# Four reorderings in a one-core encoder layer: values' copies before the next split, a pair's transposes in one run, an earlier conv mean, and first factors by ScalarE

## The chip, the cores and the metric

The kernel runs on one core of one Trainium2 chip. The metric is the device time of one execution in microseconds (us). Engines are named as in the profile: PE is TensorE (PEld its weight loads), DVE is VectorE, ACT is ScalarE, POOL is GpSimd, SP is SyncE, which issues most DMAs.

## The reference, cut to what matters

One hybrid encoder layer over 512 positions of width 2048, all float32. Names are those of the reference.

```python
xn = rms_norm(x, attn_norm_g[l])
proj = xn @ w_in[l]
u_val, u_gate, q, k, v = split(proj)              # 1024 columns each
y_conv = conformer_conv(u_val, u_gate, ...)       # u_val*sigmoid(u_gate) -> depthwise conv of 31
                                                  # -> layer norm over channels -> silu
y_na = neighborhood_attention(q, k, v, rpb[l])    # 16 heads of 64, 8 x 64 grid, windows of 8 x 16
mixed = concat([rms_norm(y_conv), rms_norm(y_na)])
x = x + mixed @ w_out[l]
up = depthwise_conv(rms_norm(x) @ w_up[l])        # width 3, 2 x 5632 columns
x = x + (silu(gate) * val) @ w_down[l]
return rms_norm(x, final_norm_g)
```

## The kernel before, in words

**Products.** Nearly all the time is matrix products. A product keeps float32 accuracy by three matmuls: each factor is split into a high part in the reduced type float32r and a low part, and `mm3` (L124 to L129) adds high by high (L127), low by high (L128) and high by low (L129) into one PSUM bank. Weights arrive by SP's DMAs in units of 128 x 1024 (`raw`). `parts` (L113 to L118) splits a unit: ACT copies the high part (`whi`, L116), and DVE subtracts for the low part (`wlo`, L117). There are four buffers of each, and `weights()` prepares units three ahead, so the split of a later unit waits until PE has read the last of an earlier one.

**Stages.** At the start the kernel loads the input and the first weights piece by piece, scales and splits them, and begins the first conv group's product. ACT and DVE share that work; the factors `g1` of the first norm are copied by DVE (L263). Then a list `ORDER` runs the input projections: conv groups ("a"), two halves of the values ("v"), and pairs of heads ("q"). A unit of a projection is eight rows of weights, that is 24 matmuls. `project_v` (L310 on) fills four PSUM banks with the values of one half; ACT then copies each bank to SBUF twice or three times, aligned and shifted (`vg` L335, `vx` L338). The first half uses three of the banks that projections use, so the next projection has to wait for the first bank's copies.

**Steps in between.** Attention and the conv group's norm are generators in the lists `steps` and `asteps`. `tick` (L136 to L144) is called after each unit and lets each list go one step further. A pair of heads goes through `scores` (into PSUM), `softmax` (tables `tab`), `turn` and `values`. `turn` (L496 to L509) transposes four tables, 16 transposes on PE (L503) in four groups of four, in the order n = 2, 3, 0, 1, and ACT copies each group out (`pt`, L508). Groups 2 and 3 have a PSUM tile each; groups 0 and 1 are the two halves of one tile, `wide`, allocated in the middle of the loop. `group_a` (L389 on) makes the conv group's mean (two matmuls, L396), subtracts it (L401), and sums squares for `rsqrt_steps` (matmuls L190 and L207); its factor `ra` is copied out of PSUM by ACT (L213) before `read_a` (L599 on) can empty the banks of the first output products (`out_half`, `po` in the profile).

**What sets the order.** The program is written in one sequence. A planner puts each engine's instructions into a queue, by their place in the program (which `shifted` moves), by what they depend on and by its own times; on the chip each engine works its queue in order and waits on semaphores. `tc.issue_after(x)` holds an instruction back behind another in the plan. `pin` (`tc.keep_in_program_order`) keeps an instruction in the order of the program among the pinned ones of its engine. PSUM has eight banks: three for tag `mm`, one for `po` (attention output, norm sums, and the output product with d == 3), two for `tr`, two for `sc`.

The second part of the kernel is the gated MLP (`up`, `down`) and the last norm. Its code is not changed.

Of the kernel before, what the change touches and what calls it, by code (L numbers as in the profile page):

```python
# [12 lines left out]
AF = mybir.ActivationFunctionType  # L13
# [17 lines left out]
KD = D // P  # L31
# [3 lines left out]
U = 8  # L35
# [31 lines left out]
def layer(ctx: ExitStack, tc: tile.TileContext, xT, xG, xw, w_a, w_in, w_v, w_out, w_up, w_down, par, tab, g3, out, last_out):  # L67
    nc = tc.nc
# [21 lines left out]
        return wpool.tile(shape, F32, tag="raw", name=name, bufs=NR)  # L90

    pin = tc.keep_in_program_order

    g1 = consts.tile([P, KD], F32, name="g1")
    prm = consts.tile([P, NPAR], F32, name="prm")
# [17 lines left out]
    def parts(raw, n):  # L113
        hi = wpool.tile([P, U * P], F32R, tag="whi", name="whi", bufs=NW)
        lo = wpool.tile([P, U * P], F32R, tag="wlo", name="wlo", bufs=NW)
        i = nc.scalar.activation(hi[:, :n], raw[:, :n], AF.Copy)  # L116
        j = nc.vector.tensor_sub(lo[:, :n], raw[:, :n], hi[:, :n].bitcast(F32))  # L117
        return hi, lo, i, j  # L118

# [4 lines left out]
    def mm3(ps, w, wk, mh, ml, start, stop):  # L124
        hi, lo = w[:2]
        a = slice(wk * P, (wk + 1) * P)
        nc.tensor.matmul(ps, hi[:, a], mh, start=start, stop=False)  # L127
        nc.tensor.matmul(ps, hi[:, a], ml, start=False, stop=False)  # L128
        return nc.tensor.matmul(ps, lo[:, a], mh, start=False, stop=stop)  # L129


    steps, asteps = [], []

    def tick(behind):
        for todo in (steps, asteps):
            while todo:  # L136
                try:
                    with tc.issue_after(behind.ins):
                        next(todo[0])
                    break  # L140
                except StopIteration:
                    todo.pop(0)
# [86 lines left out]
    ps = psa.tile([P, 2, S], F32, tag="sc", name="idle")  # L229
# [3 lines left out]
    for k in range(KD):  # L233
        if k < CH:
            raw = t4([P, U * P], "raw")
            n = S + 2 * P + (0 if k else KD)
            last = pin(nc.sync.dma_start(raw[:, :n], xw[:, k * (S + 2 * P) + (KD if k else 0):][:, :n]))
            x1.append(raw[:, :S])
            first = raw[:, S:S + 2 * P]
        else:  # L240
            if k % CH == 0:
                raw = t4([P, U * P], "raw")
            if k % CH == 0 or k == CH + 2:
                o, n = 2 * (k % CH) * P, 2 * (2 if k < 2 * CH else CH) * P
                pin(nc.sync.dma_start(raw[:, o:o + n], w_a[:, 2 * (k - CH) * P:][:, :n]))
            x1.append(t2("x"))
            last = pin(nc.sync.dma_start(x1[k], xG[k - CH]))
        h, l = t2("xh", F32R), t2("xl", F32R)
        g = g1[:, k:k + 1] if k else raw[:, n - KD:n - KD + 1]
        if k:  # L250
            pin(nc.scalar.activation(h, x1[k], AF.Copy, scale=g))
        else:
            pin(nc.vector.tensor_scalar(h, x1[k], g, None, op0=ALU.mult))
        pin(nc.vector.scalar_tensor_tensor(l, x1[k], g, h.bitcast(F32), op0=ALU.mult, op1=ALU.subtract))
        xs.append((h, l))
        if k < CH:
            early_parts(first, k)
        elif k % 2 == 0:
            early_parts(raw[:, 2 * (k % CH) * P:2 * (k % CH + 2) * P], k)
        if k in (6, 8, 10, 12):  # L260
            sum_sq(acc1, x1[k // 2 - 3], k == 6)
        if k == 0:
            pin(nc.vector.tensor_copy(g1, raw[:, n - KD:n]))  # L263
    with tc.issue_after(last.ins):
        nc.sync.dma_start(prm, par)
    a_, q_, v_ = iter(range(NC_)), iter(range(NP_)), iter(range(2))
    for step in ORDER:
        if step == "v":
            half = next(v_)
# [3 lines left out]
        i = next(a_ if step == "a" else q_)  # L273
# [22 lines left out]
    def project(n):  # L296
        ps = psm.tile([P, S], F32, tag="mm", name="pj")
        for u in range(KD // U):
            w = weights()
            for k in range(U):  # L300
                kk = u * U + k
                m = mm3(ps, w, k, xs[kk][0], xs[kk][1], kk == 0, kk == KD - 1)
            tick(m)
            while late and rstd:
                late.pop(0)()
        return ps

    vg, vx = [], []

    def project_v(half):  # L310

        if half:
            sc = psa.tile([P, 2, S], F32, tag="sc", name="pv")
            banks = [psa.tile([P, S], F32, tag="tr", name="pv", bufs=2) for _ in range(2)] + [sc[:, 0], sc[:, 1]]
        else:
            banks = [psm.tile([P, S], F32, tag="mm", name="pv") for _ in range(3)]
            banks.append(psa.tile([P, S], F32, tag="po", name="pv"))
        for u in range(KD // 2):
            wh, wl = weights()[:2]
            for k in range(2):  # L320
                kk, f = 2 * u + k, slice(k * S, (k + 1) * S)
                for t, ps in enumerate(banks):
                    xh, xl = (x[:, t * P:(t + 1) * P] for x in xs[kk])
                    nc.tensor.matmul(ps, xh, wh[:, f], start=kk == 0, stop=False)  # L324
                    nc.tensor.matmul(ps, xl, wh[:, f], start=False, stop=False)  # L325
                    m = nc.tensor.matmul(ps, xh, wl[:, f], start=False, stop=kk == KD - 1)  # L326
            tick(m)
            while late and rstd:
                late.pop(0)()
        y = rtok[0]  # L330
        vg.append([t2("vg") for _ in banks])
        vx.append([t2("vx") for _ in banks[1:]])
        with shifted(-600):
            for t, ps in enumerate(banks):
                nc.scalar.activation(vg[half][t], ps, AF.Copy, scale=y[:, t:t + 1])  # L335
                for x, rows in ((t - 1, slice(0, DH)), (t, slice(DH, P))):
                    if 0 <= x < len(vx[half]):
                        nc.scalar.activation(vx[half][x][rows], ps[rows], AF.Copy, scale=y[rows, t:t + 1])  # L338

    def project_first():  # L340

# [47 lines left out]
    def group_a():  # L389
        h, l = t2("yh", F32R), t2("yl", F32R)  # L390
        nc.scalar.activation(h, ysum[0], AF.Copy)
        nc.vector.tensor_sub(l, ysum[0], h.bitcast(F32))
        yield
        ps = psa.tile([P, S], F32, tag="po", name="st")
        for i, m in enumerate((h, l)):
            nc.tensor.matmul(ps, ones_r, m, start=i == 0, stop=i == 1)  # L396
        mu = t2("mu")
        nc.vector.tensor_scalar(mu, ps, 1.0 / CONV, None, op0=ALU.mult)
        acc = t2("acc")
        for i in range(NC_):  # L400
            nc.vector.tensor_sub(ys[i], ys[i], mu)  # L401
            sum_sq(acc, ys[i], i == 0)
            if i == NC_ // 2 - 1:
                yield
        yield
        yield
        r = yield from rsqrt_steps(acc, CONV, "rln")
        acc = t2("acc")
        for i in range(NC_):
            nc.vector.tensor_mul(ys[i], ys[i], r)  # L410
            nc.scalar.activation(ys[i], ys[i], AF.Silu, scale=pc("lng", i), bias=pc("lnb", i))
            ma.append(split(ys[i], pc("cog", i), "ma"))
            sum_sq(acc, ys[i], i == 0)
            if i % 2:
                yield
        yield
        yield
        ra.append((yield from rsqrt_steps(acc, CONV, "ra")))
# [76 lines left out]
    def turn(ts):  # L495
        pts, first = {}, True  # L496
        for n in (2, 3, 0, 1):
            if n == 0:
                wide = psa.tile([P, 2, 4, P], F32, tag="sc", name="trp")
            ps = wide[:, n] if n < 2 else psa.tile([P, 4, P], F32, tag="tr", name="trp", bufs=2)  # L500
            for i in range(2):
                for ch in range(2):
                    m = nc.tensor.transpose(ps[:, 2 * i + ch, :], ts[n][:, i, ch * P:(ch + 1) * P], ident)  # L503
                    if not first:
                        pin(m)
                    first = False
            pts[n] = t2("pt").rearrange("p (c k) -> p c k", c=4)
            nc.scalar.activation(pts[n], ps, AF.Copy)  # L508
        return pts  # L509

    def values(p, pts):
# [39 lines left out]
    p, n = -1, 0  # L551
# [392 lines left out]
    n = CH  # L944
# [47 lines left out]
    for d in range(KD):  # L992
        ps = psm.tile([P, S], F32, tag="mm", name="pd")[:, fm]
# [8 lines left out]
    sums, v, r, y, w = (sm.tile([P, CH], F32, tag="rs" + c, name="rs" + c) for c in "lvryw")  # L1002
    v, r, y, w = (t[:, :1] for t in (v, r, y, w))
# [16 lines left out]
    for g, ps in enumerate(banks):  # L1020
        for i in range(CH):
            m = nc.tensor.matmul(ps[:, i * P:(i + 1) * P], x2[g * CH + i][:, tm], ident, start=i == 0, stop=False,
                                 is_transpose=True)
            if g > 1 and i == 0:
                pin(m)
        for k in range(n):
            (hh, hl), (dh, dl) = hs[k], ws[g * CH + k]
            i = nc.tensor.matmul(ps, hh[:, tm], dh, start=False, stop=False)
# [3 lines left out]
            i = nc.tensor.matmul(ps, hl[:, tm], dh, start=False, stop=False)  # L1032
# [104 lines left out]
```

## Time and profile before

| what | value |
|---|---|
| median of 3 runs | 2025.43 us (2024.95, 2025.43, 2026.96) |
| profiled execution: its time / its span | 2026.78 us / 2025.0 us |
| PE busy in the span | 2013.7 us (99%) |
| DVE busy | 1668.0 us (82%) |
| ACT busy | 1052.0 us (52%) |
| DMA, mean | 140 GB/s |

The profile is of one execution. Its time is 1.8 us longer than its span, which runs from the first to the last recorded instruction. In the timelines, a row begins with the start in us from the span's start and the duration in us, then engine, line, operation, output and inputs, and in brackets how long the engine was idle before it and what ended that. Matmuls overlap: a duration of 0.39 us goes with a start every 0.23 us, so lost time shows in the starts rather than in the busy share.

### The profile page before, as it was taken

Reading aid. Unit: us, or ns where it says so; the run is one execution under the profiler, and the core shown is the slowest. Engines: PE = TensorE matmul, PEld = TensorE weight load, DVE = VectorE, ACT = ScalarE, POOL = GpSimd, SP = SyncE. Lnnn points to the kernel's source line nnn. Section 1 sums busy time; section 2 is a strip of 40 time slices with the busy share of each in tenths; the row PEclk is TensorE's granted clock in tenths of the full one; section 3 lists DMA queues with packets and bytes.
Section 4 is the critical chain, followed back from the end, with each engine's and each line's share of the span. In section 5 each row is a group of like instructions: output and inputs, shape, how many; then the busy total and the mean of one; then the engine's idle time right before and its main releaser. Section 6 shows DMA issues by size and latency. Waiting matters only on the chain.

```text
span 2025.0 us, 28150 instructions
## 1 busy us (share of the span) xinstructions
PE 2013.7 (99%) x10556; PEld 1721.0 (85%) x10556; DVE 1668.0 (82%) x2300; ACT 1052.0 (52%) x1686; POOL 168.7 (8%) x199
## 2 busy tenths in 40 slices
PE   9999999999999999999999999999999999999998
PEld 8788888888888998888888888888888888888887
DVE  7976888988577899888888888888888888879875
ACT  6323344466346555555555555555555555555563
POOL 0000000000001101111111111111111111110111
PEclk9999999999999999999999999999999999999999
DMA  7223333336338765565565565565565565564573
GB/s 257 94 85 93 113 94 106 106 112 231 104 119 214 198 167 146 125 146 146 125 146 146 129 142 146 127 143 146 118 153 146 125 146 146 125 144 127 146 201 132
DMA packets 98935, 284.25 MB, mean 140 GB/s; under 512 B 10992, under 2 KB 12272, under 8 KB 98800
## 3 DMA queue, kind: packets, MB, share of 16 engines
q1 hardware_dynamic: 72144, 231.07, 36.8%
q0 software_dynamic: 26656, 51.39, 16.9%
q8 instruction: 83, 1.36, 0.3%
q14 instruction: 52, 0.43, 0.1%
HBM read 227.89 MB, written 54.53 MB: 139 GB/s over the span
## 4 chain that ended last, share of the span: by engine, by line
PE 98%; DVE 1%; ACT 0%; issue 0%; DMA 0%; ACTq 0%; DVEq 0%
PE pu L759 27%; PE pu L765 14%; PE pd L129 8%; PE pd L127 8%; PE pd L128 8%; PE pj L127 6%; PE pj L129 5%; PE pj L128 5%; PE po L127 3%; PE po L129 3%; PE po L128 3%; PE pv L325 1%; PE pv L324 1%; PE pv L326 1%; PE trp L503 1%; PE pu L127 1%
## 5 line engine op out<-in xcount | busy, mean ns | idle before, releaser
L116 ACT ACTIVATE whi<-raw 128x1024 fp32r<-128x1024 f32 x364 | 384.6, 1058 | 507.8 <-PE pj L128 137.9
L117 DVE TENSOR_TENSOR wlo<-raw,whi 128x1024 fp32r<-128x1024 f32 x364 | 444.4, 1222 | 210.1 <-ACT whi L116 203.3
L759 PE MATMUL pu<-xc,whi 128*128 128x512 f32 x2352 | 580.0, 391 | 0.0
L759 PEld LDWEIGHTS pu<-xc,whi 128*128 128x128 f32 x2352 | 433.5, 188 | 83.0
L765 PEld LDWEIGHTS pu<-xc,wlo 128*128 128x128 f32 x2352 | 306.9, 191 | 14.7
L765 PE MATMUL pu<-xc,wlo 128*128 128x256 f32 x2352 | 311.4, 282 | 0.0
L129 PE MATMUL pd<-hh,wlo 128*128 128x512 f32 x640 | 250.3, 391 | 0.0
L127 PE MATMUL pd<-hh,whi 128*128 128x512 f32 x640 | 249.7, 390 | 0.0
L128 PE MATMUL pd<-hl,whi 128*128 128x512 f32 x640 | 249.1, 389 | 0.0
L913 POOL DMA_DIRECT2D x2d<-pdc x160 | 139.4, 873 | 1097.8 <-ACT pdc L912 870.9
L127 PE MATMUL pj<-xh,whi 128*128 128x512 f32 x512 | 199.6, 394 | 2.3 <-ACT vx L338 2.2
L129 PE MATMUL pj<-xh,wlo 128*128 128x512 f32 x512 | 199.2, 392 | 0.0
L128 PE MATMUL pj<-xl,whi 128*128 128x512 f32 x512 | 198.9, 391 | 0.0
L791 ACT ACTIVATE pl<-pu 128x256 f32<-128x256 f32 x294 | 109.8, 382 | 149.9 <-PE pu L759 142.8
L379 DVE SCALAR_TENSOR_TENSOR y<-ch,prm,y 128x500 f32<-128x500 f32 (+14 forms) x240 | 173.5, 740 | 4.3
L116 ACT ACTIVATE whi<-ws 128x1024 fp32r<-128x1024 f32 x132 | 139.7, 1058 | 70.9 <-PE pu L759 55.2
L117 DVE TENSOR_TENSOR wlo<-ws,whi 128x1024 fp32r<-128x1024 f32 x132 | 161.1, 1221 | 14.8 <-ACT whi L116 14.8
L129 PEld LDWEIGHTS pd<-hh,wlo 128*128 128x128 f32 x640 | 120.1, 188 | 28.5 <-DVE wlo L117 3.3
L128 PEld LDWEIGHTS pd<-hl,whi 128*128 128x128 f32 x640 | 120.2, 188 | 24.9 <-DVE hl L898 0.3
L127 PEld LDWEIGHTS pd<-hh,whi 128*128 128x128 f32 x640 | 120.4, 188 | 22.6
L912 ACT ACTIVATE pdc<-pd 128x512 f32<-128x512 f32 x160 | 93.8, 588 | 79.3 <-PE pd L129 66.2
L127 PEld LDWEIGHTS pj<-xh,whi 128*128 128x128 f32 x512 | 96.6, 189 | 23.5 <-ACT vx L338 2.6
(220 smaller groups left out, 2728.9 us busy)
## 6 DMA issues: line engine op xcount, KB each, us to landing
raw<-in_w_up SPq DMA_DIRECT2D x176, 512.0 KB, 3.8
raw<-in_w_down SPq DMA_DIRECT2D x88, 512.0 KB, 4.0
x2d<-pdc POOLq DMA_DIRECT2D x160, 256.0 KB, 4.9
raw<-in_w_in SPq DMA_DIRECT2D x60, 512.0 KB, 3.8
raw<-in_w_out SPq DMA_DIRECT2D x32, 512.0 KB, 3.7
raw<-in_w_v SPq DMA_DIRECT2D x16, 512.0 KB, 3.7
tab<-in_tab SPq DMA_DIRECT2D x32, 256.0 KB, 5.1
x<-in_xT SPq DMA_DIRECT2D x16, 256.0 KB, 5.4
```

Source lines behind the costliest of these rows:

```text
L116: i = nc.scalar.activation(hi[:, :n], raw[:, :n], AF.Copy)
L117: j = nc.vector.tensor_sub(lo[:, :n], raw[:, :n], hi[:, :n].bitcast(F32))
L127: nc.tensor.matmul(ps, hi[:, a], mh, start=start, stop=False)
L128: nc.tensor.matmul(ps, hi[:, a], ml, start=False, stop=False)
L129: return nc.tensor.matmul(ps, lo[:, a], mh, start=False, stop=stop)
L324: nc.tensor.matmul(ps, xh, wh[:, f], start=kk == 0, stop=False)
L379: nc.vector.scalar_tensor_tensor(y[:, a:b], h[:, a + j - PAD:b + j - PAD], prm[:, o + j:o + j + 1], y[:, a:b], op0=ALU.mult, op1=ALU.add)
L759: i = nc.tensor.matmul(ps, w[0][:, k * P:(k + 1) * P], comb[c][k], start=k == 0, stop=stop and k == ks[-1])
L765: i = nc.tensor.matmul(ps[:, H:], w[1][:, k * P:(k + 1) * P], comb[c][k][:, :H], start=False, stop=stop and k == U - 1)
L791: nc.scalar.activation(to, ps, AF.Copy)
L912: nc.scalar.activation(t, ps, AF.Copy)
L913: nc.gpsimd.dma_start(xd[d], t, accum_op=ALU.add)
```

## The change

Four edits:

1. After the copies of `project_v`, a mark (`copied`) makes the next split of a unit on ACT a pinned instruction. The copies are pinned too, so the copies stand before that split in ACT's queue.
2. After the transposes of `turn`, a mark (`turned`) makes the first matmul of the next `mm3` a pinned one. The transposes of a pair are pinned already, so this matmul comes after all 16.
3. `group_a` yields "mid" after the split of the sum. `project` calls `tick(m, mid=True)` after the fifth row of weights of each unit, and only a step that stands at "mid" is taken there. A third empty `yield` keeps the later steps at the units where they were.
4. `g1` is copied by ACT rather than DVE.

```diff
     pin = tc.keep_in_program_order
+    copied, turned = [], []
...
         i = nc.scalar.activation(hi[:, :n], raw[:, :n], AF.Copy)
+        if copied:
+            copied.pop()
+            pin(i)
...
-        nc.tensor.matmul(ps, hi[:, a], mh, start=start, stop=False)
+        m = nc.tensor.matmul(ps, hi[:, a], mh, start=start, stop=False)
+        if turned:
+            turned.pop()
+            pin(m)
...
-    steps, asteps = [], []
-
-    def tick(behind):
+    steps, asteps, amid = [], [], [False]
+
+    def tick(behind, mid=False):
+
         for todo in (steps, asteps):
-            while todo:
+            while todo and mid == (todo is asteps and amid[0]):
                 try:
                     with tc.issue_after(behind.ins):
-                        next(todo[0])
+                        at = next(todo[0])
+                    if todo is asteps:
+                        amid[0] = at == "mid"
                     break
...
         if k == 0:
-            pin(nc.vector.tensor_copy(g1, raw[:, n - KD:n]))
+            pin(nc.scalar.activation(g1, raw[:, n - KD:n], AF.Copy))
...
                 m = mm3(ps, w, k, xs[kk][0], xs[kk][1], kk == 0, kk == KD - 1)
+                if k == U // 2:
+                    tick(m, mid=True)
             tick(m)
...
-                nc.scalar.activation(vg[half][t], ps, AF.Copy, scale=y[:, t:t + 1])
+                pin(nc.scalar.activation(vg[half][t], ps, AF.Copy, scale=y[:, t:t + 1]))
                 for x, rows in ((t - 1, slice(0, DH)), (t, slice(DH, P))):
                     if 0 <= x < len(vx[half]):
-                        nc.scalar.activation(vx[half][x][rows], ps[rows], AF.Copy, scale=y[rows, t:t + 1])
+                        pin(nc.scalar.activation(vx[half][x][rows], ps[rows], AF.Copy, scale=y[rows, t:t + 1]))
+        copied.append(half)
...
         nc.vector.tensor_sub(l, ysum[0], h.bitcast(F32))
-        yield
+        yield "mid"
...
-        yield
-        yield
+        for _ in range(3):
+            yield
         r = yield from rsqrt_steps(acc, CONV, "rln")
...
             nc.scalar.activation(pts[n], ps, AF.Copy)
+        turned.append(pts)
         return pts
```

## The prediction

> **What bounds the kernel now.** I read the page first (busy times, then the chain that ended last), then the waits of TensorE and of its weight loads, then timelines around the places that the edits touch.
>
> ```profile
> span 2025.0 us, 28150 instructions
> PE 2013.7 (99%) x10556; PEld 1721.0 (85%) x10556; DVE 1668.0 (82%) x2300; ACT 1052.0 (52%) x1686; POOL 168.7 (8%) x199
> ...
> PE 98%; DVE 1%; ACT 0%; issue 0%; DMA 0%; ACTq 0%; DVEq 0%
> ...
> PE pj L127 <- ACT vx L338: 2.2, 1, 2.2
> PEld trp L503 <- ACT pt L508: 2.7, 8, 0.4
> ```
>
> The chain is PE for 98%: nothing counts unless it moves PE's matmuls. Of PE's own waits the one long one is 2.2 us, once, on a values' copy. The last row is a warning: eight times, as many as there are pairs, a weight load for a transpose waited for a copy `pt`. So the edits are priced by what they do to gaps between matmul starts.
>
> **Edit 1, values' copies.**
>
> ```profile
> 87.35 0.39 PE L326 MATMUL pv<-wlo,xh 128*128 128x512 f32 x1
> ...
> 94.15 0.39 PE L326 MATMUL pv<-wlo,xh 128*128 128x512 f32 x1
> 96.73 0.50 PE L127 MATMUL pj<-xh,whi 128*128 128x512 f32 x1 [2.19 <-ACT vx L338]
> ...
> 97.78 0.63 PE L128 MATMUL pj<-xl,whi 128*128 128x512 f32 x1
> ...
> 101.18 0.39 PE L127 MATMUL pj<-xh,whi 128*128 128x512 f32 x1
> 94.35 1.06 ACT L116 ACTIVATE whi<-raw 128x1024 fp32r<-128x1024 f32 x1 [4.38 <-PE pv L325]
> 95.32 0.67 ACT L335 ACTIVATE vg<-pv,rsy 128x512 f32<-128x512 f32 x1
> 96.00 0.68 ACT L338 ACTIVATE vx<-pv,rsy 64x512 f32<-64x512 f32 x1
> 97.80:101.10 3.30, 3.30 (x9) 2.62 (x8) 3.19 (x6) 3.24 (x6) 0.00 (x0) 0.50 0.44 146
> ```
>
> From 87.35 to 94.15 are 30 matmuls, 0.227 us each: the cadence used below. The next was due at 94.38 and started at 96.73, 2.35 late, plus some 0.11 for a first load that nothing covered: 2.46. ACT stood idle for 4.38 us in front of a split that waits for the unit's end, with the copies behind it. The first bank's last matmul starts nine places before 94.15, at 92.11, and ends at 92.50. With the copies ahead, its two (0.67 and 0.68) end near 93.9, before 94.38: the wait goes. The split comes after ten copies, near 99.2 rather than 94.35, and DVE's low part later still; PE needs that unit three units of 24 matmuls after 94.38, at 110.7, so its cover is about ten us. The second half's copies already stand ahead of their split: nothing there.
>
> After the gap the granted clock was 0.50 (third number from the end of the last row), and from 97.78 to 101.18 eight matmuls took 0.425 each: 1.59 us more. The Trainium skill ("TensorE: Matmul & The Clock Gate", "Why this matters for your kernels") asks only that idle gaps stay under about 3 us. By that rule this gap would cost no clock, and the sum below would rise by the 1.59; the trace shows the half clock after a 2.2 us gap, so the row decides.
>
> **Edit 4, first factors.**
>
> ```profile
> 2.03 0.20 ACT L228 ACTIVATE idle<-ones 128x1 f32<-128x1 f32 x1
> 5.58 0.17 DVE L263 COPY g<-raw 128x16 f32<-128x16 f32 x1
> 5.79 0.72 ACT L251 ACTIVATE xh<-raw,g 128x512 fp32r<-128x512 f32 x1 [1.31 <-DVE g L263]
> 6.11 0.62 PE L129 MATMUL pj<-xh,wlo 128*128 128x512 f32 x2
> 6.42 0.40 ACT L223 ACTIVATE whi<-raw 128x256 fp32r<-128x256 f32 x1
> 6.87 0.73 PE L127 MATMUL pj<-xh,whi 128*128 128x512 f32 x2
> raw<-in_xw SPq DMA_DIRECT2D x1, 384.0 KB, 3.8
> ```
>
> After L129 at 6.11 and 6.34 the next matmul was due at 6.57, came at 6.87 and its pair took 0.11 longer: 0.41. On ACT a copy of 128x16 isn't shown; it lies between 0.20 (128x1) and 0.40 (128x256). ACT is free at 4.48 (5.79 less 1.31), so it ends before the second input piece, issued near 1.2, lands near 5.0. Then `xh` starts 0.8 earlier and the split ends near 6.0, before 6.57. Gain 0.41, between 0 and 0.41.
>
> **Edit 3, the mean.**
>
> ```profile
> 433.39 0.39 PE L129 MATMUL pj<-xh,wlo 128*128 128x512 f32 x1
> 433.99 1.05 PE L190 MATMUL st<-ones,acc 128*128 128x1 f32 x8 [0.21 <-DVE acc L170]
> ```
>
> L190 was due at 433.62: 0.37 lost to a sum of squares that DVE finished late. With subtractions and squares up to half a unit (2.7 us) earlier this goes: gain 0.37, between 0 and 0.4.
>
> **Edit 2, transposes.**
>
> ```profile
> 258.07 1.06 ACT L116 ACTIVATE whi<-raw 128x1024 fp32r<-128x1024 f32 x1 [4.38 <-PE pj L128]
> 258.11 1.48 PE L503 MATMUL trp<-ident,tab 128*128 128x128 f32 x12
> 259.04 1.56 ACT L508 ACTIVATE pt<-trp 128x512 f32<-128x512 f32 x3
> 259.34 0.48 PE L127 MATMUL pj<-xh,whi 128*128 128x512 f32 x1
> ...
> 260.65 0.66 PE L503 MATMUL trp<-ident,tab 128*128 128x128 f32 x4
> 261.06 0.48 PE L129 MATMUL pj<-xh,wlo 128*128 128x512 f32 x1
> ...
> 309.31 0.39 PE L127 MATMUL pj<-xh,whi 128*128 128x512 f32 x1
> 309.62 0.66 PE L503 MATMUL trp<-ident,tab 128*128 128x128 f32 x4
> ...
> 307.99 1.58 ACT L508 ACTIVATE pt<-trp 128x512 f32<-128x512 f32 x3 [5.11 <-PE trp L503]
> ```
>
> The last four transposes (n = 1) write the other half of the tile `wide` from which ACT copies n = 0, and they began 0.05 after that third copy ended (259.04 + 1.56 = 260.60, then 260.65; 309.57, then 309.62). Five matmuls of the projection filled the time in the first pair, four in the second. In the changed program PE's queue holds 16 transposes in a row in five pairs (first, second, third, seventh, eighth). ACT's copies stay where they are, so the 13th transpose still begins at 260.65, PE idles 1.2 us from 259.42, and the displaced matmuls follow: after 261.06 the stream is behind by exactly their number. Four pairs by 5 x 0.227 = 1.13, one by 4 x 0.227 = 0.91: 5.44 lost. The joining of two runs saves nothing, as ACT sets the end. Lower bound 0, if the copies came 1.2 earlier; upper bound about 1.3 a pair (6.5). The fourth and fifth pairs keep five matmuls in between.
>
> The sixth pair changes otherwise. Its four last transposes now stand behind the 24 matmuls of the first output product (before: behind 24 of the last key projection), which then come after them. PE's count stays, but two things follow. The sums L207 now stand right behind the third output product, and the fourth, which takes the same single bank `po`, right behind them; ACT's queue holds a split that waits for that third product ahead of the copy `ao`, which frees the bank for L207.
>
> ```profile
> 499.75 0.58 ACT L524 ACTIVATE ao<-po 128x512 f32<-128x512 f32 x1
> 501.10 0.62 PE L207 MATMUL st<-dg,ones 128*128 128x512 f32 x2
> 501.76 0.60 ACT L213 ACTIVATE ra<-st 128x512 f32<-128x512 f32 x1 [0.77 <-PE st L207]
> 502.69 1.07 ACT L116 ACTIVATE whi<-raw 128x1024 fp32r<-128x1024 f32 x1 [0.33 <-PE po L128]
> 502.71 0.39 PE L127 MATMUL po<-mah,whi 128*128 128x512 f32 x1
> ```
>
> Before, `ao` went ahead of that split (499.75, 502.69), and five matmuls lay between L207 and the next user of the bank at 502.71, behind `ra`'s end at 502.36. After: let the third product's last matmul start at t. The high part's last reader ends at t - 0.23 + 0.39; the split starts near t + 0.20, `ao` 0.97 later (as 94.35 to 95.32) and ends 0.60 on, so L207 starts near t + 1.81 instead of t + 0.23: 1.58. The second L207 starts 0.23 after the first and ends 0.39 later; `ra` starts 0.04 after that and takes 0.60; with 0.05 more the fourth product starts 1.08 after the second L207 instead of 0.23: 0.86. Together 2.44, between 0 (if `ao` isn't held) and 3.2 (ACT later by one more 0.7 copy).
>
> **The sum.** Against the profiled execution (2026.78, of which the span is 2025.0 and 1.78 lies outside, unchanged): -2.46 - 1.59 - 0.41 - 0.37 + 5.44 + 2.44 = +3.05, so 2029.8. The runs shown lie at 2024.95 and 2025.43 and at 2026.96; the profiled time is 1.4 to 1.8 above the lower two, about the half clock's 1.59. I estimate that those two ran without it. From the median the sum is then +4.64: 2030.1. I take 2030.0. From the second part of the kernel I expect no change: its chain is PE before and after, and all of it starts later.
>
> **The rivals.**
> - *The half clock follows the new gaps.* For: it followed one of 2.2 us. Against: the five are 1.2, and the sixth pair's 1.58 and 0.86 are parted by two sums. Each time costs 1.59: 2031.6 with the sixth pair alone, up to 2039.5 with five more. By the skill's rule of 3 us it comes at none.
> - *The sixth pair costs nothing,* because ACT reaches `ao` sooner: 2030.0 - 2.44 = 2027.6. Against it stands the queue.
> - *The other side: the 13th transpose no longer waits.* If the third copy ends before the twelfth transpose does, the five runs cost nothing, and the time is 2030.0 - 5.44 = 2024.6, not slower. It decides at 1.2 us: so much earlier must ACT finish. For it: a split fills ACT from 258.07 right ahead of the copies. Against: in the second pair no split did, and the wait ended just as exactly on the copy.
> - *All as the edits say,* nothing lost: 2022.2, not quite 0.2% down.
>
> **How the numbers follow.** Forecast 0.60 (2029.3 to 2030.8); half clock 0.20, of it 0.13 for the sixth pair alone; sixth pair free 0.11; no wait in the runs 0.06; all gained 0.03. The range 2027.5 to 2032.0 holds 0.60 + 0.13 + 0.11 = 0.84. About 0.2% (4.05 us) can be told from no change; slower by more starts at 2029.48. The forecast lies close above it: four fifths of its 0.60 and the half clock's 0.20 give 0.68 slower. Faster by more (under 2021.4) gets 0.02, and 0.30 is left for same.
>
> **What would show it.** (Lines as before the change.) Right: no wait of `pj` on `vx` and clock 1.00 near 98; five new waits of PE transposes on `pt`, about 1.2 each; new waits of `st` L207 on `ao` (1.6) and of the next output product on `ra` (0.9), near 500; `xh` starting near 5.0. Wrong: 16 transposes through in 1.9 us without a gap, or a clock of 0.50 anywhere between 255 and 545.

## The result, and the profile after

| | before | after |
|---|---|---|
| median (range, runs) | 2026.67 us (2024.95 to 2026.96, 9) | 2030.77 us (2029.58 to 2032.02, 9) |
| ratio after / before | | 1.0024, 95% interval 1.0015 to 1.0034 |
| profiled execution: time / span | 2026.78 / 2025.0 us | 2031.87 / 2029.8 us |

The changed kernel is slower by about 4 us, as forecast, and the time lies inside the range. Both kernels' times fall into two groups. Before, three of the nine lie within 0.5 of 2025.2 and six near 2026.7. After, five lie at 2029.58 to 2030.77 and four at 2031.4 to 2032.0. The groups come from the halved TensorE clock, which follows a gap in some executions and not in others: after, the mean granted clock is 0.999 in the five and 0.998 in the four. The two medians come from different groups, the upper one before and the lower one after. Group against group the change costs more than the 4.1 between the medians: 5.6 in the lower (medians 2024.96 and 2030.53) and 5.1 in the upper (2026.70 and 2031.84).

Page of the kernel after: the span, the busy times, the chain that ended last.

```profile
span 2029.8 us, 28156 instructions
PE 2013.8 (99%) x10556; PEld 1721.3 (85%) x10556; DVE 1667.7 (82%) x2299; ACT 1051.5 (52%) x1687; POOL 168.9 (8%) x199
...
PE 99%; ACT 1%; DMA 0%; issue 0%; SPq 0%; DVE 0%; ACTq 0%
```

PE has the same 10556 matmuls and the same busy time (2013.7 before). The 4.8 us of span are gaps and clock, and the waits say where. Waits of PE, after (total us, times, longest):

```profile
PE trp L516 <- ACT pt L521: 5.1, 5, 1.1
PE st L217 <- ACT ao L538: 1.4, 1, 1.4
...
PE po L131 <- ACT ra L223: 0.7, 1, 0.7
```

The wait of `pj` on `vx` (2.2) is gone. In its place stand five waits of the 13th transpose, one of the sums L217 on `ao` and one of the next output product on `ra`. (Lines have moved: transposes L516, `pt` L521, `mm3` L131, L135 and L136, sums L217.)

**The start.** Timeline after:

```profile
4.41 0.20 ACT L273 ACTIVATE g<-raw 128x16 f32<-128x16 f32 x1
5.09 0.72 ACT L261 ACTIVATE xh<-raw,g 128x512 fp32r<-128x512 f32 x1 [0.48 <-DMA raw<-in_xw]
...
6.46 0.63 PE L131 MATMUL pj<-xh,whi 128*128 128x512 f32 x2
...
6.99 0.72 ACT L261 ACTIVATE xh<-raw,g 128x512 fp32r<-128x512 f32 x1 [0.86 <-DMA raw<-in_xw]
...
8.07 0.73 PE L131 MATMUL pj<-xh,whi 128*128 128x512 f32 x2
...
9.69 0.39 PE L131 MATMUL pj<-xh,whi 128*128 128x512 f32 x1
```

The first `xh` starts 0.70 earlier (5.09 for 5.79), but the second waits for its input piece until 6.99. The matmuls are 0.41 ahead of the kernel before at 6.46 and 0.31 at 8.07; at 9.69 (before: 9.78) 0.09 is left.

**The values.** Timeline after, PE and ACT, and a stretch with its busy time and clock:

```profile
94.06 0.39 PE L338 MATMUL pv<-wlo,xh 128*128 128x512 f32 x1
94.28 0.39 PE L131 MATMUL pj<-xh,whi 128*128 128x512 f32 x1
...
93.15 0.69 ACT L350 ACTIVATE vx<-pv,rsy 64x512 f32<-64x512 f32 x1
...
98.96 2.00 ACT L117 ACTIVATE whi<-raw 128x1024 fp32r<-128x1024 f32 x2
96.73:101.10 4.37, 4.37 (x21) 1.00 0.00 0
```

The projection follows the last value matmul at the usual cadence, the split starts at 98.96 (forecast 99.2), and the clock stays at 1.00.

**A pair.** Timeline after, first pair:

```profile
253.89 1.47 PE L516 MATMUL trp<-ident,tab 128*128 128x128 f32 x12
256.43 0.66 PE L516 MATMUL trp<-ident,tab 128*128 128x128 f32 x4 [1.07 <-ACT pt L521]
256.84 0.47 PE L131 MATMUL pj<-xh,whi 128*128 128x512 f32 x1
...
253.86 1.06 ACT L117 ACTIVATE whi<-raw 128x1024 fp32r<-128x1024 f32 x1 [4.38 <-PE pj L135]
254.82 1.56 ACT L521 ACTIVATE pt<-trp 128x512 f32<-128x512 f32 x3
```

ACT's third copy ends at 254.82 + 1.56 = 256.38, and the 13th transpose starts 0.05 later, as before. What has changed is that PE idles for the 1.07 us ahead of it, from the end of the 12th, where projection matmuls stood before.

**The sixth pair.** Timeline after, PE and ACT, then two stretches:

```profile
500.51 0.39 PE L136 MATMUL po<-mah,wlo 128*128 128x512 f32 x1
502.30 0.73 PE L217 MATMUL st<-dg,ones 128*128 128x512 f32 x2 [1.41 <-ACT ao L538]
503.73 0.79 PE L131 MATMUL po<-mah,whi 128*128 128x512 f32 x1 [0.69 <-ACT ra L223]
...
500.71 1.06 ACT L117 ACTIVATE whi<-raw 128x1024 fp32r<-128x1024 f32 x1 [1.78 <-PE po L135]
501.67 0.58 ACT L538 ACTIVATE ao<-po 128x512 f32<-128x512 f32 x1
...
499.93:503.35 3.42, 1.70 (x7) 1.00 0.92 346
503.35:506.76 3.41, 3.04 (x7) 0.50 0.53 159
```

The split does stand ahead of `ao` in ACT's queue, and PE waits first for `ao` (1.41) and then for `ra` (0.69). Then the clock is 0.50 for 3.41 us, in this execution.

### The profile page after: what moved, and what is told of

It is laid out like the page before. It is cut to its first block, busy times and chain, and to the rows that moved or that the text cites. A ratio compares the mean times of both kernels' runs of the same rounds, so it can differ in the third digit from the quotient of the medians.

```text
span 2029.8 us, 28156 instructions
## 1 busy us (share of the span) xinstructions
PE 2013.8 (99%) x10556; PEld 1721.3 (85%) x10556; DVE 1667.7 (82%) x2299; ACT 1051.5 (52%) x1687; POOL 168.9 (8%) x199
## 4 chain that ended last, share of the span: by engine, by line
PE 99%; ACT 1%; DMA 0%; issue 0%; SPq 0%; DVE 0%; ACTq 0%
PE pu L773 26%; PE pu L779 14%; PE pd L136 8%; PE pd L131 8%; PE pd L135 8%; PE pj L131 6%; PE pj L135 6%; PE pj L136 6%; PE po L131 3%; PE po L135 3%; PE po L136 3%; PE pv L337 1%; PE pv L338 1%; PE pv L336 1%; PE po L532 1%; PE pu L131 1%
## 5 line engine op out<-in xcount | busy, mean ns | idle before, releaser
L136 PE MATMUL pd<-hh,wlo 128*128 128x512 f32 x640 | 250.4, 391 | 0.0
L131 PE MATMUL pd<-hh,whi 128*128 128x512 f32 x640 | 249.7, 390 | 0.0
L135 PE MATMUL pd<-hl,whi 128*128 128x512 f32 x640 | 249.1, 389 | 0.0
L131 PE MATMUL pj<-xh,whi 128*128 128x512 f32 x512 | 198.6, 393 | 0.1
L135 PE MATMUL pj<-xl,whi 128*128 128x512 f32 x512 | 198.1, 390 | 0.0
L136 PE MATMUL pj<-xh,wlo 128*128 128x512 f32 x512 | 198.1, 390 | 0.0
L136 PEld LDWEIGHTS pd<-hh,wlo 128*128 128x128 f32 x640 | 120.1, 188 | 28.5 <-DVE wlo L121 3.3
L135 PEld LDWEIGHTS pd<-hl,whi 128*128 128x128 f32 x640 | 120.2, 188 | 25.0 <-DVE hl L912 0.3
L131 PEld LDWEIGHTS pd<-hh,whi 128*128 128x128 f32 x640 | 120.4, 188 | 22.6
L131 PEld LDWEIGHTS pj<-xh,whi 128*128 128x128 f32 x512 | 96.1, 188 | 20.7 <-ACT whi L233 0.5
```

Source lines behind the costliest of these rows:

```text
L131: m = nc.tensor.matmul(ps, hi[:, a], mh, start=start, stop=False)
```

## The experiments

The edits are numbered as in the change. Ratios are to the kernel before, timed on the same chip. Its times there fall into the same two groups, near 2025.3 and 2026.8.

**Edit 1 alone.**

```diff
+        if copied:
+            copied.pop()
+            pin(i)
...
-                nc.scalar.activation(vg[half][t], ...)
+                pin(nc.scalar.activation(vg[half][t], ...))    # vx too
+        copied.append(half)
```

> The kernel before with edit 1 alone (the values' copies ahead of the next split). Theory: the one wait of the projection on the copy vx (2.46 us with its uncovered load) goes, and with it the half clock behind it (1.59 us), so the times are one group near 2022.6 (2025.1, the lower times of before, less 2.46), about 4.0 under before's median, and the granted clock is 1.0 near 98 us. Rival, half clock not tied to the wait: only 2.46 is gained, the times stay in two groups 1.6 apart near 2022.6 and 2024.2. Rival, the split that is now ten copies later comes too late for the unit that needs it: a new wait near 110 us, and less than 2 us gained.

Measured: 2022.76 us (2022.54 to 2023.09, 11 runs), ratio 0.9984 (0.9975 to 0.9993), one group. The wait and the half clock behind it went together: 2.5 below the median of the lower group and 4.1 below that of the upper. No new wait came.

**Edit 2 alone.**

```diff
+        m = nc.tensor.matmul(ps, hi[:, a], mh, start=start, stop=False)
+        if turned:
+            turned.pop()
+            pin(m)
...
+        turned.append(pts)
```

> The kernel before with edit 2 alone (16 transposes of a pair in one run). Theory: five gaps ahead of the 13th transpose cost 5.4 us in all, the sixth pair's two waits (on ao and on ra) 2.4 us; the wait on vx stays. Against before's median of 2026.7 that is 2034.5, and up to 1.6 more in runs with a half clock near 503 us: 2034.5 to 2036.1. Rival, the gaps arise only together with the other edits: the time stays within 3 us of before (under 2029.7).

Measured: 2038.55 us (2037.13 to 2038.83, 5 runs), ratio 1.0059 (1.0047 to 1.0072). That is 2.5 above the upper end of what was expected. Waits of PE in this kernel:

```profile
PE trp L507 <- ACT pt L512: 5.1, 5, 1.1
...
PE st L211 <- DVE dg L205: 1.7, 1, 1.7
PE st L211 <- ACT ao L529: 1.4, 1, 1.4
...
PE st L194 <- DVE acc L174: 0.7, 1, 0.7
```

The five waits and the one on `ao` are those of the changed kernel. Two more came with them, near 437 and 444. The sum of squares L194 waits 0.7 for `acc`, where it had waited 0.2, and a sum waits 1.7 for `dg`, which DVE makes behind a low part.

**The changed kernel without edit 2** (only the line `turned.append(pts)` left out).

> The changed kernel without edit 2 (edits 1, 3 and 4 kept). Theory: edit 2 costs 5.4 in five pairs, 2.4 in the sixth and 1.5 of half clock there in many runs, and the others gain 2.5 + 1.6 + 0.5 + 0.1; so 2022.1 (2025.1 less 2.46, 0.46 and 0.10), in one group, all 16 of the waits of transposes short as before. Rival, the loss is made in the start or by the moved mean: the time stays above 2027. Rival, the wait behind the values' copies and the gaps trade with each other (ACT merely shifted): 2024 to 2027.

Measured: 2022.33 us (2021.57 to 2022.98, 11 runs), ratio 0.9981 (0.9972 to 0.9990). PE has no wait left but the one at the start. Edit 2 carries the whole loss: 8.4 us between the two medians.

**The copy of n = 0 later**, all four edits kept.

```diff
-            pts[n] = t2("pt").rearrange("p (c k) -> p c k", c=4)
-            nc.scalar.activation(pts[n], ps, AF.Copy)
+            made_ps[n] = ps
+            for c in {0: (), 1: (0, 1)}.get(n, (n,)):
+                pts[c] = t2("pt").rearrange("p (c k) -> p c k", c=4)
+                nc.scalar.activation(pts[c], made_ps[c], AF.Copy)
```

> The changed kernel with all four edits, but ACT's copy of group n = 0 is written after the transposes of group n = 1, so that nothing reads the tile wide between its two halves. Theory: the gap ahead of the 13th transpose is the wait for the copy of the other half of the same tile, made by the order of these two steps and not by 16 transposes in a row; all 16 go through in about 2 us without a gap in all eight pairs, the two copies follow, and the sixth pair falls back to the order that it had before: 2021.5 (2022.1 less about 0.08 for each pair whose two runs are joined), between 2021.3 and 2022.6. Rival, 16 in a row wait for ACT anyway (for the copies of the groups n = 2 and 3 or of the pair before): 2027 to 2031. Rival, the copy of n = 0, up to 0.5 later, holds up the products of the attention: 2022.6 to 2026.

Measured: 2021.02 us (2020.50 to 2021.84, 9 runs), ratio 0.9976 (0.9967 to 0.9986). First pair, PE and ACT:

```profile
253.91 1.91 PE L516 MATMUL trp<-ident,tab 128*128 128x128 f32 x16
255.57 0.47 PE L131 MATMUL pj<-xh,whi 128*128 128x512 f32 x1
...
254.84 2.10 ACT L523 ACTIVATE pt<-trp 128x512 f32<-128x512 f32 x4
```

All 16 transposes go through in 1.91 us while ACT still copies. Sixteen in a row thus need no wait. The wait came from writing the second half of `wide` behind the copy of its first half: with the same tiles and another order of these two steps it is gone. This kernel is faster than the kernel before and than the changed one. All its eight pairs have 16 transposes in a row, where the mark had joined five. Against the profile of the run without edit 2, each join saves some 0.14 us (0.08 was expected); that can account for the 0.3 by which the time lies under its expected range.

**The same without edit 2** (the late copy, `turned.append(pts)` left out).

> As the run with the late copy, but without edit 2: no pin, only the copy of n = 0 written after the transposes of n = 1 (and edits 1, 3, 4). Theory: the order of the copy alone lets all 16 transposes stand in a row, so that the mark adds nothing: the same as that run, 2021.0, within 0.4. Rival, the mark is what joins them, and without it the four last transposes drift behind matmuls as before: near 2022.2, the time without edit 2.

Measured: 2021.02 us (2020.48 to 2021.60, 8 runs), ratio 0.9973 (0.9963 to 0.9983). The mark adds nothing once the copy stands later: without it, too, all eight pairs have 16 transposes in a row.

**Edit 2 in all pairs but the sixth.**

```diff
-        turned.append(pts)
+        if len(aos) != 5:
+            turned.append(pts)
```

> The changed kernel with the mark of edit 2 left out for the sixth pair alone. Theory: the order around the first output products is that of before, both waits (1.57 on ao, 0.86 on ra) and the half clock behind them go, and the five gaps of the other pairs stay: 2027.6 (2022.2 plus 5.4), in one group, without a clock of 0.50 between 255 and 545 although five idle stretches of 1.1 us are left. Rival, any idle gap of over 1 us can halve the clock: two or more groups, 1.5 us apart, up to 2030. Rival, the waits of the norm's sums come from edit 3 and not from the transposes: near 2030.

Measured: 2027.47 us (2027.01 to 2028.06, 11 runs), ratio 1.0006 (0.9997 to 1.0015), one group. Timeline of this kernel near the first output products:

```profile
499.79 0.39 PE L131 MATMUL po<-mah,whi 128*128 128x512 f32 x1
500.01 0.62 PE L217 MATMUL st<-dg,ones 128*128 128x512 f32 x2
500.47 0.40 PE L135 MATMUL po<-mal,whi 128*128 128x512 f32 x1
```

The sums go through between two matmuls without a wait. The sixth pair alone costs 3.3 us of the medians: its two waits, and the half clock in some executions. Against the run without edit 2, the five remaining gaps cost 2027.47 - 2022.33 = 5.1.

**Edit 3 alone.**

```diff
-        yield
+        yield "mid"
...
+                if k == U // 2:
+                    tick(m, mid=True)
```

> The kernel before with edit 3 alone (the mean of the conv group in the middle of a unit). Theory: the one wait of the norm's sum near 433 goes: 0.4 to 0.5 less, lower group of times near 2024.9 instead of 2025.3, upper group 1.5 above it. Rival, the five-row tick moves other work of DVE into the way: a new wait and a time above 2025.6 in the lower group.

Measured: 2024.91 us median of 11, ratio 0.9996 (0.9987 to 1.0005). Six runs lie at 2024.45 to 2024.91 and five at 2026.09 to 2026.40; of the kernel before, ten of 24 lie at 2025.11 to 2025.45 and the rest above 2026.5. The lower groups' medians are 2024.78 and 2025.29: 0.5 less.

**Edits 2 and 3.**

> Edits 2 and 3 without 1 and 4. Edit 2 alone came to 2038.55, some 2.4 over the forecast for it, with two more waits of sums at 436.7 (0.83 lost) and at 443.7 (1.93 lost, behind a low part on DVE). Theory: these two come from the transposes moving while the conv norm's steps stay at a unit's end, and edit 3 moves those steps out of the way: 2.8 less than edit 2 alone, so 2034.3 to 2035.8. Rival, they come with edit 2 whatever edit 3 does, and edits 1 or 4 removed them: 2037 to 2038.6.

Measured: 2033.14 us (2032.78 to 2036.08, 5 runs), ratio 1.0037 (1.0025 to 1.0050). That is 1.2 under the expected range. The lowest run lies 4.4 under the lowest with edit 2 alone. The waits on `dg` and on `acc` are gone, so edit 3 is what keeps them out of the changed kernel. The rest of the 4.4 is, as far as the profiles tell, clock: the profiled run here took 2036.08 with two half-clock periods, that of edit 2 alone 2037.13 with one. With 1.5 for each they would be 2033.1 and 2035.6, some 2.5 apart.

**Edit 4 alone** (`g1` copied by ACT).

> The kernel before with edit 4 alone (first factors copied by ScalarE). Theory of the forecast: 0.41 less, lower group of times near 2024.9 instead of 2025.3. Rival, read from the changed kernel's profile, where the third input piece landed only at 6.98: the next piece sets the pace instead, and 0.1 is gained: 2025.2.

Measured: 2026.29 us median of 11 (2024.61 to 2026.98), ratio 0.9999 (0.9990 to 1.0008). Lower groups: medians 2024.98 and 2025.14; upper groups: 2026.39 and 2026.75. So 0.2 to 0.4 is gained, between the two theories, and not well resolved.

**The copy of n = 0 made twice, three and four times** in the changed kernel, to lengthen the gap.

```diff
-            nc.scalar.activation(pts[n], ps, AF.Copy)
+            for _ in range(2 if n == 0 else 1):    # 3, 4
+                nc.scalar.activation(pts[n], ps, AF.Copy)
```

> The changed kernel, but ACT makes the copy of group n = 0 twice over (the same result), so that each of the five waits ahead of the 13th transpose grows from 1.1 by one copy of some 0.5 to 1.6 us. Theory: each of the five gaps costs its length and no clock, 2.6 more in five pairs (the sixth pair's order changes too, 2.4 either way): 2030.8 to 2033.4. Rival, idle stretches of 1.6 halve the clock: a clock of 0.50 behind some of the five, 1.5 each, up to 2041.

> As before with the copy of n = 0 made three times: waits of 2.1 to 2.2 us, about as long as the wait on vx in the kernel before. Theory: such a gap halves the clock for 3.41 us when it falls well inside one period of 3.41 us counted from the start, so in about half of the gaps: two or three of five in a profile; 5.2 for the longer gaps and 1.5 for each half clock: 2036 to 2041. Rival, by a rule that only gaps over about 3 us do it (the Trainium skill, TensorE: Matmul & The Clock Gate, Why this matters for your kernels): none of the five, and 2033.6 to 2036.

> As before with the copy of n = 0 made four times: waits of 2.6 to 2.7 us. Theory: more of the five gaps than with three copies (three to five) are followed by a clock of 0.50 for 3.41 us: 7.8 for the longer gaps and 1.5 for each: 2041 to 2047. Rival, by the rule of about 3 us none: 2036 to 2039.

Measured: 2033.62, 2046.36 and 2052.82 us (4 runs each), ratios 1.0038 (1.0024 to 1.0051), 1.0100 (1.0086 to 1.0114) and 1.0130 (1.0114 to 1.0145). One copy lengthens a gap by 0.63, not 0.5. With two, the five waits are up to 1.7 us long and none halves the clock in the profile. With three (up to 2.3), three of the five do, and with four (up to 3.0), four of five. The first total lies 0.2 above its expected range, the others 5 to 6 above theirs. In these two the sixth pair's wait on `ao` grew too, to 3.1 and 3.3 us, with 6.83 us of half clock behind it. With four copies a sum also waited 1.7 for `dg`, and one of the four half clocks lasted 6.83 us.

Why some gaps and not others? Below, the stretches begin and end on a grid of 3.41 us counted from the start of the full clock in each profile. Columns: stretch, its length, PE busy (matmuls), granted clock, DMA share, GB/s. The kernel before, then edit 4 alone, both around the wait on `vx`:

```profile
94.33:97.75 3.42, 1.23 (x5) 1.00 0.09 10
97.75:101.16 3.41, 3.41 (x9) 0.50 0.44 144
```

```profile
94.74:98.15 3.41, 1.72 (x7) 1.00 0.27 35
98.15:101.56 3.41, 3.41 (x17) 1.00 0.29 119
```

Three copies, the first and the last gap:

```profile
255.00:258.42 3.42, 1.09 (x10) 1.00 0.29 61
258.42:261.83 3.41, 3.41 (x10) 0.50 0.23 93
...
558.79:562.20 3.41, 1.43 (x9) 1.00 0.44 145
562.20:565.62 3.42, 3.42 (x10) 0.50 0.04 13
```

Four copies, the second and the last:

```profile
310.01:313.42 3.41, 1.50 (x9) 1.00 0.00 0
313.42:316.83 3.41, 3.41 (x17) 1.00 0.00 0
...
566.01:569.42 3.41, 1.44 (x9) 1.00 0.54 154
569.42:572.83 3.41, 3.41 (x10) 0.50 0.02 5
```

Two copies, the fourth gap:

```profile
511.94:515.35 3.41, 1.72 (x16) 1.00 0.18 28
515.35:518.76 3.41, 3.41 (x17) 1.00 0.89 320
```

The same 2.2 us wait cost a half clock where it fell inside one period (1.23 busy) and none where it straddled two (1.72). In these rows a period with at most 1.44 us of busy time is followed by a half-clock one, and a period with 1.50 or more is not; nor is one with 1.52 around the wait on `vx` with edit 2 alone (92.99 to 96.40). Transposes count as busy here: the 1.72 us with two copies are all transposes, and the clock stayed at 1.00. A gap of 1.1 leaves 2.3 busy at worst, out of reach of this limit. The sixth pair does not fit it: 1.70 busy was followed by 0.50 in the changed kernel, and 1.60 in the run with edits 2 and 3 (504.31 to 507.72). What is different there, besides the two gaps in one period, was not tried.

## Why the prediction was right, point by point

The measured terms compare the starts of the same matmuls in the two profiles.

| step | forecast | measured |
|---|---|---|
| edit 1, wait and half clock | -4.05 | -4.12 |
| edit 4 | -0.41 | -0.10 in the profiles, -0.2 to -0.4 in the times |
| edit 3 | -0.37 | -0.46 in the profiles, -0.5 in the times |
| edit 2, five pairs | +5.44 | +5.41 |
| edit 2, sixth pair, waits | +2.44 | +2.42 |
| half clock at the sixth pair | 0 (chance 0.13) | +1.6 in the profiled run |
| sum | +3.05 | +4.8 |

The sum of +4.64 over the median then known (2025.43) was for executions without a half clock in either kernel. Between such executions the change costs 5.6, or 5.2 against the 2025.3 of the larger sets of before: 0.6 to 1.0 more than forecast. Edit 4 accounts for up to 0.3 of it; the rest stays open. That the two medians lie only 4.1 apart, nearer to the forecast, is luck: before's median lies in the group with a half clock and the changed kernel's in the group without.

- **Edit 1: right, with its cause shown.** Alone it gives the expected 2022.7, in one group.
- **Edit 4: the term was mis-sized.** The forecast took the ACT queue's start as the limit and did not ask when the later input pieces land. That varies from run to run: the second `xh` waited for its piece until 6.99 in the changed kernel and started at 5.97, without such a wait, in the run with edit 4 alone.
- **Edit 3: right alone, incomplete beside edit 2.** The wait of the sum of squares near 433 went. What the forecast did not see is that the same edit keeps 1.7 us on `dg`, and a longer wait on `acc`, out of the way when the transposes are joined. The sum still came out, because edit 3 is part of the change and those two waits never arise in it. The forecast had not looked for them, so this was luck.
- **Edit 2: right.** Five waits, five sizes, and two waits of the sixth pair within 0.03 of the working. The run with the late copy shows that the cause is the shared tile's order; the run without the sixth pair separates the two parts.
- **The rivals.** The thirteenth transpose does wait; the sixth pair is not free; not all is gained. The first rival, a half clock at the sixth pair, holds in the profiled run and, by the groups, in about four of nine. By the prediction's own sign of being wrong, a clock of 0.50 between 255 and 545, that step failed there: its reason, that two sums part the two waits, does not hold, as the first wait and the start of the second fell into one period of 3.41 us (499.93 to 503.35). The range had room for one half clock, so the time stayed inside. It does not explain why the median lies 0.8 above the forecast, as the median's own execution has a granted clock of 0.999. The estimate that the lower times of before were those without a half clock is borne out: edit 1 alone leaves one group.

## What to carry to other kernels

A pin that keeps a run together moves work out of a hole; price what the displaced work was covering before you pin. Here the hole was a copy of one half of a PSUM tile standing between writes of both halves, and changing the order of that copy, not of the matmuls, gave 9.75 us against the changed kernel (2030.77 and 2021.02). When a queue's order is changed, look at every place where the mark takes effect: one of the eight pairs, with another neighbour on its bank, cost as much as two of the others (2.4 us against some 1.1 each), before any loss of clock.

## What the runs showed of the hardware that was not expected

- The clock is judged by periods of 3.41 us, not by the length of a gap. Of the gaps with three copies three in five, and with four copies four in five, were followed by a half clock; single waits of 1.1 and of 1.7 never were in the profiles. The half-clock rows above begin on the 3.41 us grid: 258.42 and 562.20 lie 89 periods apart.
- The Trainium skill ("TensorE: Matmul & The Clock Gate", "What's actually happening") says that a free-running window of 3413 ns sets the clock; the 3.41 us periods here agree. Its "Why this matters for your kernels" asks only for idle gaps under about 3 us. The rows disagree: a wait of 2.2 us was enough when it lay inside one period.
- A kernel with one such gap has two times, 1.5 apart, and its median says mostly which of them came more often: 2025.55 in one set of 25 runs of the kernel before, 2026.68 in another of 24.
